# Weight splits of the up products in product order, each behind an evacuation three products back

## The chip, the cores and the metric

The kernel runs on one core of a Trainium2 chip. The metric is the device time of one execution in microseconds (us). The engines are TensorE (PE in the profile), VectorE (DVE), ScalarE (ACT), GpSimd (POOL) and SyncE (SP), each with its own in-order instruction stream; SP and GpSimd also issue the DMAs.

## The reference

One sequence of 512 rows and width 1024 goes through four layers, all in float32. The first two add a mixer (forgetting attention, then a gated recurrence) and a SwiGLU; the last two another pair of mixers and a convolutional FFN. Each FFN begins with an "up" GEMM from 1024 to 2 x 2816 columns; the change touches these four.

```
def swiglu_ffn(h, w_in, w_out):
    gate, up = jnp.split(jnp.einsum('bsd,df->bsf', h, w_in), 2, axis=-1)
    return jnp.einsum('bsf,fd->bsd', jax.nn.silu(gate) * up, w_out)

def conv_ffn(h, w_up, conv_w, conv_b, w_down):
    u = h @ w_up
    up = jnp.pad(u, ((0, 0), (CONV_WIDTH - 1, 0), (0, 0)))
    conv = conv_b
    for j in range(CONV_WIDTH):
        conv = conv + conv_w[j] * up[:, j:j + s]
    a, g = jnp.split(conv, 2, axis=-1)
    return (jax.nn.silu(a) * g) @ w_down
```

Before each FFN stands an RMS norm: the rows are divided by the root of the mean of their squares over the 1024 columns.

## The kernel before

Every float32 GEMM is done as three passes over split operands: a high part (a cast to the matmul's own type, `hi`) and a low part (`lo = raw - hi`). For weights, `pump` emits the splits in the order of a list of `Spec`s: a CAST on ScalarE (L237), a subtraction on VectorE (L238), and for some an adding DMA on GpSimd (L240), which adds another block of the weight from DRAM into the same raw tile, so that the next split of that tile is that of a sum. `pump` goes on as long as a slot (W0 to W2, and W3 during the up GEMMs) and the raw tiles are there.

The four up GEMMs (up0 and up1 for SwiGLU, up2 and up3 for the convolution; at about 300 to 540, 1020 to 1260, 1600 to 1845 and 2200 to 2445 us) are done for each pair of column tiles j (11 of them) by a scheme that needs seven products instead of eight. Products p1 and p2 use plain weight blocks, p5, p6, p3, p7, p4 blocks that are sums built up by the adding DMAs: p6 is cast from the raw tile of p5 after one such DMA, and so on. A product is 24 matmuls. `up_first` does p1 and p2 of j = 0 to 3 while the last norm still runs; `up` then does pairs (0,1) and (2,3), and from j = 4 a loop: p5(j), p1(j+1), p3(j), p6(j), p2(j+1), p7(j), p4(j). p3 accumulates on the PSUM bank of p5, and p7 on that of p6; so p3 waits until ScalarE has copied p5's result out (L904 in SwiGLU, L947 in conv), and p7 until it has copied p6's (L906, L949).

The evacuations (`swiglu_evac`, `conv_evac`) are the copies and adds that assemble the outputs: copies on ScalarE, adds on VectorE (L908, L951, L957) and GpSimd (L915, L954); in conv then the convolution (ScalarE `u` and `s`, L931, VectorE L932 and L933), a silu (L962) and a product on GpSimd (L965). Names in the trace: `W` is a split slot, `raw` a raw tile, `hid` the outputs, `a`, `s`, `g`, `m` the activations' splits and PSUM banks.

The order of PE's instructions is written by hand. On the other engines a scheduler lists the instructions by readiness and priority when the kernel is built; `high_priority` raises some of them.

`norm_chain` makes the norm in front of each FFN in two halves of 256 rows: VectorE updates `h` in four pieces of two column blocks, ScalarE squares each (L435), VectorE adds up the first three (L437), and `rstd` multiplies what is left as four operands (two halves of `sums`, two of the last square) with a vector of 1/1024 on PE (L399). `combine` then makes, for the second half, the sums of the activations (s1 to s4, a22) and their splits, in a fixed sequence on VectorE.

Of the kernel before, what the change touches and what calls it, by code (L numbers as in the profile page):

```python
# [8 lines left out]
F32 = mybir.dt.float32  # L9
# [49 lines left out]
class Spec:  # L59
# [1 line left out]

    def __init__(self, tag, nk, nc, slots, early, raw, loads=(), prep=None, add=None, ends=()):
        self.tag, self.nk, self.nc, self.slots, self.early = tag, nk, nc, slots, early
        self.raw, self.loads, self.prep, self.add, self.ends = raw, loads, prep, add, ends


class Net:
    def __init__(self, ctx, tc, t):  # L70
        self.ctx, self.tc, self.nc, self.t = ctx, tc, tc.nc, t
        nc = tc.nc
        e = ctx.enter_context
        self.base = e(tc.tile_pool(name="base", bufs=1))
        self.wp = e(tc.tile_pool(name="wp", bufs=1))
        self.nrm = e(tc.tile_pool(name="nrm", bufs=2))
        self.sm = e(tc.tile_pool(name="sm", bufs=4))
        self.psg = e(tc.tile_pool(name="psg", bufs=4, space=PSUM))
        self.psa = e(tc.tile_pool(name="psa", bufs=2, space=PSUM))
        self.psm = e(tc.tile_pool(name="psm", bufs=2, space=PSUM))  # L80
        self.drp = e(tc.tile_pool(name="drp", bufs=2, space=bass.MemoryType.DRAM))

        b = self.base
        self.h = b.tile([P, NC, S], F32, tag="h", name="h")
        self.ident = b.tile([P, P], F32, tag="ident", name="ident")
        make_identity(nc, self.ident)
        self.invn = b.tile([P, 1], F32, tag="invn", name="invn")
        nc.vector.memset(self.invn, 1.0 / D)
        self.mhalf = b.tile([P, 32], F32, tag="mhalf", name="mhalf")
        nc.vector.memset(self.mhalf, -0.5)  # L90
        self.slot_at = {f"W{i}": self.wp.tile([P, 2048], F32R, tag=f"W{i}", name=f"W{i}") for i in range(3)}
        self.free = {"W0", "W1", "W2"}
        self.raw_at = {f"raw{i}": self.wp.tile([P, 1024], F32, tag=f"raw{i}", name=f"raw{i}") for i in range(3)}
        self.raw_free = list(self.raw_at)
        self.raws = {}
        self.specs, self.loads = [], []
        self.adds, self.hold = [], False
        self.n_dma = self.n_split = self.n_got = self.n_raw = 0
        self.pe_time, self.later, self.events = 0.0, [], set()
        self.loaded = {}  # L100
# [116 lines left out]
    def pump(self, most=99):  # L217
        nc = self.nc
        for _ in range(most):
            if self.n_split == len(self.specs):  # L220
                break
            self.load_more()
            s = self.specs[self.n_split]
            slot = next((x for x in s.slots if x in self.free), None)
            if slot is None or any(k not in self.raws for k in s.loads):
                return
            if any(key in s.loads for key, *_ in self.adds):
                self.flush(self.last_pow)
            self.free.discard(slot)
            if s.prep:  # L230
                out, x, y, eng = s.prep
                getattr(nc, eng).tensor_add(self.raws[out][1], self.raws[x][1], self.raws[y][1])
            n = s.nk * s.nc
            reg = self.slot_at[slot]
            hi, lo = reg[:, :n], reg[:, 1024 : 1024 + n]
            raw = self.raws[s.raw][1][:, :n]
            nc.scalar.copy(hi, raw)  # L237
            (nc.gpsimd if s.early else nc.vector).tensor_sub(lo, raw, hi.bitcast(F32))  # L238
            if s.add is not None:
                nc.gpsimd.dma_start(raw.rearrange("p (k c) -> p k c", k=s.nk), s.add, accum_op=ALU.add)  # L240
            for k in s.ends:
                self.raw_free.append(self.raws.pop(k)[0])
            r = dict(k=s.nk)
            self.loaded[self.n_split] = Chunk(
                slot, hi.rearrange("p (k c) -> p k c", **r), lo.rearrange("p (k c) -> p k c", **r), s.nk)
            self.n_split += 1
        self.load_more()
# [142 lines left out]
            nc.scalar.activation(sq[:, :n], src, AF.Square)  # L390
            eng.tensor_add(acc[:, cols], acc[:, cols], sq[:, :n])  # L391

    def rstd(self, parts):

        nc = self.nc
        st = self.mbank()
        for j in range(2):
            for i, a in enumerate(parts):
                nc.tensor.matmul(st[:, j : j + 1], a[:, j * P : (j + 1) * P], self.invn, start=i == 0,  # L399
                                 stop=i == len(parts) - 1)  # L400
        with self.tc.high_priority(400):
            v = self.sm.tile([P, 2], F32, tag="v", name="v")
            nc.vector.tensor_scalar_add(v, st[:, 0:2], EPS)
            r = self.sm.tile([P, 2], F32, tag="r", name="r")
            self.last_pow = nc.gpsimd.tensor_tensor(r, v, self.mhalf[:, 0:2], ALU.pow)
        return r
# [9 lines left out]
    def norm_chain(self, acc, half, gain, pool=None, y=None, acc_y=None, work=None):  # L416


        nc = self.nc
        cols = slice(half * HS, (half + 1) * HS)  # L420
        if y is not None:
            yield 2.6
            r = self.rstd([acc_y[:, cols]])
            if half and work is not None:
                self.flush(self.last_pow)
            yield 2.0
            R = self.spread(r)[:, :HS].unsqueeze(1).to_broadcast([P, 2, HS])
            with self.tc.high_priority(400):
                sums = pool.tile([P, 2, HS], F32, tag="sums", name="sums", bufs=2)
                for c in range(0, NC, 2):  # L430
                    tmp = y[:, c : c + 2, cols]
                    hv = self.h[:, c : c + 2, cols]
                    nc.vector.tensor_mul(tmp, tmp, R)
                    (nc.vector.tensor_sub if work is None else nc.vector.tensor_add)(hv, hv, tmp)
                    nc.scalar.activation(tmp if c else sums, hv, AF.Square)  # L435
                    if c in (2, 4):
                        nc.vector.tensor_add(sums, sums, tmp)  # L437
            parts = [a[:, i] for a in (sums, tmp) for i in range(2)]
            yield 7.0
        else:  # L440
            yield 5.4 if half and work is not None else 2.6
            parts = [acc[:, cols]]
        r = self.rstd(parts)
        if half and work is not None:
            self.flush(self.last_pow)
        yield 1.4 if y is not None else 2.8 if half and work is not None else 2.0
        R = self.spread(r)
        with self.tc.high_priority(400):
            if work is not None:
                with self.tc.manual_schedule(engines={mybir.EngineType.DVE}):  # L450
                    self.combine(pool, work, half, gain, R)
                return
            for c in range(NC):
                tmp = self.nrm.tile([P, HS], F32, tag="tmp", name="tmp", bufs=3)
                nc.vector.scalar_tensor_tensor(tmp, self.h[:, c, cols], gain[:, c : c + 1], R[:, :HS], ALU.mult,
                                               ALU.mult)
                self.split(tmp, self.res(c, 0, half), self.res(c, 1, half))

    def combine(self, pool, work, half, gain, R):
# [19 lines left out]
        if not half:  # L479
            rest = []  # L480
            for c in range(NC):
                norm(c)
                rest.append(high("a12" if c >= 4 else "a11", c % 4, work[:, c, cols], 1))
                if c > 1:
                    rest.pop(0)()
            for low in rest:
                low()
            return
        g = (0, 2)
        a11, a12 = [work[:, k : k + 2, lo] for k in g], [work[:, 4 + k : 6 + k, lo] for k in g]  # L490
        a21, a22 = [work[:, k : k + 2, hi] for k in g], [work[:, 4 + k : 6 + k, hi] for k in g]
# [19 lines left out]
        s2[1]()  # L511
        s3 = [high("s3", g[i], a21[i]) for i in range(2)]
        last = [high("a22", g[i], a22[i]) for i in range(2)]
        for low in s3 + last:
            low()


    def columns(self, pool):
# [232 lines left out]
    def plan_up(self, tag, w, engines=None):  # L751
# [11 lines left out]

        def spec(j, p, raw, **kw):
            slots = early[j > 0] if (j, p) in first else W[:3] if (j, p) in rest[-3:] else W
            self.specs.append(Spec(tag, 4, 256, slots, False, raw, **kw))

        for j, p in first + rest:
            e = j < self.EARLY
# [55 lines left out]
    def up_first(self, tag, st):  # L825

        st["x"], st["y"], st["c11"] = {}, {}, {}
        for j, p in self.up_order()[0]:
# [3 lines left out]
            else:  # L832
                st["y"][j] = self.abank()
                self.product(tag, p, st["y"][j])
                if j < 2:
                    c = st["c11"][j] = self.nrm.tile([P, S], F32, tag="sq", name="c11")
                    self.c11(st["x"][j], st["y"].pop(j), c)

    def c11(self, x, y, out):
        self.nc.scalar.copy(out, x)  # L840
# [2 lines left out]
    def up(self, tag, st, evac):  # L843
# [9 lines left out]
        for j, p in rest:  # L853
# [25 lines left out]
            done.add((j, p))  # L879
            if p in (3, 6) and {(j, 3), (j, 6)} <= done:  # L880
                first(j, 3, z.pop(j))

    @staticmethod
    def halves(a):
# [1260 lines left out]
```

## Time and profile before

| | us |
|---|---|
| median of 3 runs | 2580.16 |
| lowest, highest | 2576.74, 2585.74 |
| profiled execution | 2584.16 |
| its span | 2582.3 |

In the span PE is busy 96%, the weight loads (PEld, beside it) 85%, VectorE 59%, ScalarE 45%, GpSimd 21%. Of the chain that ended last 43% lies on PE, 6% on VectorE, 3% on DMA and 2% on ScalarE. The rows further down are from the timelines, where a row is start, duration, engine, line, operation, output<-inputs, shapes, count, and in brackets the idle time of the engine before it and what ended that; and from a table of stretches.

### The profile page before, as it was taken

To read this page: it belongs to the slowest core of one execution; us is meant where nothing else is said; L and a number is where in the kernel's file an instruction comes from. 1 tells how busy PE (TensorE), PEld (TensorE's weight loads), DVE (VectorE), ACT (ScalarE), POOL (GpSimd) and SP (SyncE) were. 2 spreads that over 40 slices of the span, in tenths; PEclk is the share of its full clock that TensorE was granted. 3 is DMA by queue.
4 is the path that set the end of the run, shared out by engine and by line. 5 is a ranking of instruction groups with operands and counts; after the bars stand their busy time and mean duration, and the time that the engine had idled before them with its cause. 6 is when DMAs were issued, how large, how long until landed. Compare 5 with 4: busy or idle time off the path is not lost.

```text
span 2582.3 us, 40752 instructions
## 1 busy us (share of the span) xinstructions
PE 2467.4 (96%) x16477; PEld 2205.8 (85%) x16477; DVE 1527.4 (59%) x2400; ACT 1168.2 (45%) x1920; POOL 550.1 (21%) x500
## 2 busy tenths in 40 slices
PE   8999889999999998799999989899999999999999
PEld 6778889998898988799988759899888768989978
DVE  5766565563555555655625675787834445697841
ACT  4545445553232324455533553566622433466731
POOL 0000133310011111233101221455300000264400
PEclk9999989999999999899999999999999999999999
DMA  4223379944112123799531213989541223889741
GB/s 136 83 74 99 105 136 191 184 108 127 50 58 74 58 90 94 142 191 186 111 127 62 65 58 106 160 172 175 119 129 57 65 58 106 181 167 177 146 142 29
DMA packets 304886, 297.00 MB, mean 115 GB/s; under 512 B 11645, under 2 KB 294875, under 8 KB 304699
## 3 DMA queue, kind: packets, MB, share of 16 engines
q1 hardware_dynamic: 210235, 197.57, 25.0%
q0 software_dynamic: 94384, 96.81, 24.1%
q8 instruction: 129, 2.11, 0.3%
q14 instruction: 58, 0.48, 0.1%
q10 hardware_dynamic: 80, 0.03, 0.0%
HBM read 292.24 MB, written 2.13 MB: 114 GB/s over the span
## 4 chain that ended last, share of the span: by engine, by line
PE 43%; DVE 6%; DMA 3%; issue 3%; ACT 2%; POOL 1%; ACTq 0%; DVEq 0%; POOLq 0%
PE g L334 34%; PE a L334 4%; DMA raw<-in_ffn_w_up_dram 3%; DVE W L238 2%; ACT W L237 1%; PE m L334 1%; PE m L1900 1%; DVE u L932 1%; DVE s L932 1%; DVE s L933 0%; ACT s L931 0%; PE a L1883 0%; PE a L1209 0%; DVE R L173 0%; DVE u L933 0%
## 5 line engine op out<-in xcount | busy, mean ns | idle before, releaser
L238 DVE TENSOR_TENSOR W<-raw,W 128x1024 fp32r<-128x1024 f32 x455 | 573.2, 1263 | 458.9 <-ACT W L237 456.1
L237 ACT CAST W<-raw 128x1024 fp32r<-128x1024 f32 x455 | 472.4, 1040 | 603.6 <-PE g L334 272.7
L334 PE MATMUL g<-R,W 128*128 128x512 f32 (+2 forms) x3048 | 685.0, 375 | 7.8 <-DVE W L238 4.8
L334 PEld LDWEIGHTS g<-R,W 128*128 128x128 f32 (+1 forms) x3048 | 511.4, 190 | 105.1 <-issue 6.1
L334 PE MATMUL g<-s,W 128*128 128x256 f32 x3840 | 479.2, 284 | 27.6 <-ACT hid L947 13.6
L334 PEld LDWEIGHTS g<-s,W 128*128 128x128 f32 x3840 | 467.9, 191 | 32.5 <-ACT hid L947 16.5
L334 PE MATMUL g<-W,R 128*128 128x256 f32 (+1 forms) x1224 | 233.9, 337 | 0.0
L334 PEld LDWEIGHTS g<-W,R 128*128 128x128 f32 x1224 | 181.8, 191 | 25.3 <-issue 6.7
L334 PE MATMUL a<-a,W 128*128 128x256 f32 x1536 | 196.1, 283 | 3.5 <-DVE c L841 2.2
L334 PEld LDWEIGHTS a<-a,W 128*128 128x128 f32 x1536 | 188.8, 190 | 4.3 <-DVE c L841 2.4
L240 POOL DMA_DIRECT2D raw<-in_ffn_w_in_dram x78 | 100.4, 1289 | 228.5 <-DVE W L238 212.4
L240 POOL DMA_DIRECT2D raw<-in_ffn_w_up_dram x78 | 103.5, 1368 | 121.5 <-DVE W L238 114.5
L334 PE MATMUL g<-a,W 128*128 128x256 f32 x864 | 109.6, 282 | 0.3
L965 POOL TENSOR_TENSOR hid<-u,s 128x512 f32<-128x512 f32 x44 | 82.6, 1887 | 118.4 <-ACT s L962 111.8
L334 PE MATMUL g<-R,R 128*128 128x256 f32 (+1 forms) x792 | 107.0, 291 | 0.7 <-ACT ya L657 0.7
L334 PEld LDWEIGHTS g<-a,W 128*128 128x128 f32 x864 | 105.6, 189 | 1.1 <-DVE a L475 0.9
L238 DVE TENSOR_TENSOR X<-raw,X 128x1024 fp32r<-128x1024 f32 (+1 forms) x46 | 49.6, 1085 | 95.6 <-ACT X L237 95.6
L391 POOL TENSOR_TENSOR acc<-acc,sq 128x512 f32<-128x512 f32 x19 | 30.0, 1581 | 355.1 <-ACT sq L390 355.0
L334 PEld LDWEIGHTS g<-R,R 128*128 128x128 f32 x792 | 101.2, 195 | 2.7 <-ACT ya L657 1.1
L334 PE MATMUL g<-R,X 128*128 128x256 f32 (+1 forms) x576 | 94.0, 320 | 0.0
L334 PEld LDWEIGHTS g<-R,X 128*128 128x128 f32 x576 | 83.1, 190 | 7.8
L237 ACT CAST X<-raw 128x1024 fp32r<-128x1024 f32 (+1 forms) x46 | 42.9, 937 | 98.6 <-PE g L334 72.3
(413 smaller groups left out, 3451.2 us busy)
## 6 DMA issues: line engine op xcount, KB each, us to landing
raw<-in_ffn_w_in_dram POOLq DMA_DIRECT2D x88, 512.0 KB, 6.3
raw<-in_ffn_w_up_dram POOLq DMA_DIRECT2D x88, 512.0 KB, 6.3
raw<-in_ffn_w_in_dram SPq DMA_DIRECT2D x76, 512.0 KB, 4.9
raw<-in_ffn_w_up_dram SPq DMA_DIRECT2D x76, 512.0 KB, 4.8
raw<-in_ffn_w_out_dram SPq DMA_DIRECT2D x40, 512.0 KB, 3.5
raw<-in_ffn_w_down_dram SPq DMA_DIRECT2D x40, 512.0 KB, 4.0
raw<-in_hgrn_w_in_dram SPq DMA_DIRECT2D x32, 512.0 KB, 4.1
raw<-in_fox_w_in_dram SPq DMA_DIRECT2D x24, 512.0 KB, 3.8
```

Of the source, the lines that this page charges most:

```text
L237: nc.scalar.copy(hi, raw)
L238: (nc.gpsimd if s.early else nc.vector).tensor_sub(lo, raw, hi.bitcast(F32))
L240: nc.gpsimd.dma_start(raw.rearrange("p (k c) -> p k c", k=s.nk), s.add, accum_op=ALU.add)
L334: self.nc.tensor.matmul(*args, **kw, **(dict(skip_group_check=True) if skip else {}))
L391: eng.tensor_add(acc[:, cols], acc[:, cols], sq[:, :n])
L932: nc.vector.scalar_tensor_tensor(u[:, 1:], src[:, : S - 1], w(1), u[:, 1:], ALU.mult, ALU.add)
L965: nc.gpsimd.tensor_mul(hid[:, t], u, s)
L1900: mm(po[i * 64 : i * 64 + 64, h * HS : (h + 1) * HS], q[:, 2 * b + h, ck * 64 : (ck + 1) * 64], state[h], start=True, stop=True)
```

## The change

A `Spec` of an up GEMM carries `up`, and for the products 4 to 7 `summed`. p3's block, a plain one, isn't counted as summed.

- `pump` stops at a summed split while `n_split > n_evac + 3`. `n_evac` is set to `n_got - 1` in the new `evacuated()`, which is called behind each product's evacuation and pumps again.
- The CASTs of the up splits are chained in product order on ScalarE (`issue_after`), and the subtractions get the priority 200.
- In `norm_chain` VectorE adds all three later squares and then the two halves of the sum into `acc`; `rstd` takes this one operand.
- `combine` hands the low parts of s3 and a22 back to be issued behind it, outside its priority and its fixed sequence.

```
@@ pump
             if slot is None or any(k not in self.raws for k in s.loads):
                 return
+            if s.summed and self.n_split > self.n_evac + 3:
+                return
@@
-            nc.scalar.copy(hi, raw)
-            (nc.gpsimd if s.early else nc.vector).tensor_sub(lo, raw, hi.bitcast(F32))
+            with self.tc.issue_after(self.last_hi.ins) if s.up and self.last_hi else ExitStack():
+                self.last_hi = nc.scalar.copy(hi, raw)
+            with self.tc.high_priority(self.FIRST) if s.up else ExitStack():
+                (nc.gpsimd if s.early else nc.vector).tensor_sub(lo, raw, hi.bitcast(F32))
@@ rstd
-            for i, a in enumerate(parts):
-                nc.tensor.matmul(st[:, j : j + 1], a[:, j * P : (j + 1) * P], self.invn, start=i == 0,
-                                 stop=i == len(parts) - 1)
+            nc.tensor.matmul(st[:, j : j + 1], acc[:, j * P : (j + 1) * P], self.invn, start=True, stop=True)
@@ norm_chain
-                    if c in (2, 4):
+                    if c:
                         nc.vector.tensor_add(sums, sums, tmp)
-            parts = [a[:, i] for a in (sums, tmp) for i in range(2)]
+                nc.vector.tensor_add(acc[:, cols], sums[:, 0], sums[:, 1])
@@ combine
-        for low in s3 + last:
-            low()
+        return s3 + last
@@ plan_up
-            self.specs.append(Spec(tag, 4, 256, slots, False, raw, **kw))
+            self.specs.append(Spec(tag, 4, 256, slots, False, raw, up=True, summed=p > 3, **kw))
@@ up_first, up: behind each product's evacuation
+            self.evacuated()
+    def evacuated(self):
+        self.n_evac = self.n_got - 1
+        self.pump()
```

In the loop of up2, ScalarE's rows of one group before, from the cast of p5 to the copy that p3 waits for. In order the casts are those of p5, p1, p3, p6 and p2.

```order
L237 CAST W3_14896<-raw3_14904 128x1024
L949 COPY hid_14900<-g_15890 128x2x256
L237 CAST W2_90<-raw5_14906 128x1024
L237 CAST W0_88<-raw2_93 128x1024
L953 COPY g_16002<-g_15890 128x2x256
L237 CAST W1_89<-raw3_14904 128x1024
L931 ACTIVATE u_16290<-hid_14900,ccol_409 128x512
L931 ACTIVATE u_16300<-hid_14900,ccol_409 128x512
L931 ACTIVATE s_16285<-g_16002,ccol_409 128x512
L931 ACTIVATE s_16295<-g_16002,ccol_409 128x512
L237 CAST W3_14896<-raw4_14905 128x1024
L947 COPY hid_14900<-g_16305 128x2x256
```

The same place in the changed kernel (L243 is the CAST, L962 the copy of p6, L966 of p7, L960 of p5):

```order
L962 COPY hid_14868<-g_15858 128x2x256
L243 CAST W1_89<-raw3_14872 128x1024
L243 CAST W3_14864<-raw5_14874 128x1024
L243 CAST W2_90<-raw2_93 128x1024
L966 COPY g_15964<-g_15858 128x2x256
L243 CAST W0_88<-raw3_14872 128x1024
L944 ACTIVATE u_16255<-hid_14868,ccol_409 128x512
L944 ACTIVATE u_16265<-hid_14868,ccol_409 128x512
L944 ACTIVATE s_16250<-g_15964,ccol_409 128x512
L944 ACTIVATE s_16260<-g_15964,ccol_409 128x512
L243 CAST W1_89<-raw4_14873 128x1024
L960 COPY hid_14868<-g_16270 128x2x256
```

The copy of p6 now stands ahead of p5's CAST, and that CAST goes to W1 (the slot that p2 reads) instead of W3 (that of p6); W3 now takes p1. The rest keeps its order.

In the beginning of up2, ScalarE's rows around the two c11 copies before:

```order
L237 CAST W0_88<-raw1_92 128x1024
L390 ACTIVATE sq_14613<-h_78 128x256
L237 CAST W1_89<-raw2_93 128x1024
L390 ACTIVATE sq_14617<-h_78 128x256
L840 COPY c11_14678<-g_14620 128x512
L237 CAST W2_90<-raw0_91 128x1024
L840 COPY c11_14782<-g_14681 128x512
L474 CAST a22_14187<-yb_14195 128x2x256
```

The same place after:

```order
L243 CAST W0_88<-raw1_92 128x1024
L397 ACTIVATE sq_14581<-h_78 128x256
L243 CAST W1_89<-raw2_93 128x1024
L397 ACTIVATE sq_14585<-h_78 128x256
L852 COPY c11_14641<-g_14588 128x512
L852 COPY c11_14747<-g_14644 128x512
L243 CAST W2_90<-raw0_91 128x1024
L481 CAST a22_14155<-yb_14163 128x2x256
```

The CAST of the first summed split has moved behind the second c11 copy.

## Rows read from the trace of the kernel before

**Rows 1.** Stretches: start:end, us, busy PE PEld DVE ACT POOL, PEclk, DMA share, GB/s

```profile
280.00:380.00 100.00, 81.55 (x592) 80.21 (x591) 62.17 (x99) 44.76 (x72) 19.84 (x17) 0.86 0.63 138
...
1000.00:1100.00 100.00, 81.92 (x594) 79.68 (x593) 62.89 (x97) 45.16 (x72) 25.04 (x20) 0.88 0.70 147
1600.00:1720.00 120.00, 109.34 (x860) 107.11 (x859) 96.05 (x112) 66.09 (x90) 55.84 (x37) 0.96 0.87 174
1720.00:1840.00 120.00, 116.49 (x971) 115.46 (x970) 96.91 (x111) 79.89 (x109) 56.02 (x38) 1.00 0.86 163
2200.00:2320.00 120.00, 109.25 (x894) 106.80 (x893) 98.20 (x119) 67.84 (x93) 55.28 (x36) 1.00 0.88 177
2320.00:2440.00 120.00, 115.99 (x967) 114.97 (x965) 97.28 (x111) 79.05 (x107) 57.18 (x39) 1.00 0.88 166
```

**Rows 2.** Timeline of TensorE in the loop of up2, one group of products

```profile
1729.63 5.98 PE L334 MATMUL g<-s,W 128*128 128x256 f32 x48 [0.15 <-ACT hid L947]
1735.45 3.01 PE L334 MATMUL a<-a,W 128*128 128x256 f32 x24
1738.30 3.02 PE L334 MATMUL g<-s,W 128*128 128x256 f32 x24
...
1750.61 1.57 PE L334 MATMUL g<-s,W 128*128 128x256 f32 x11 [0.73 <-ACT hid L947]
```

**Rows 3.** Timeline of ScalarE in the same group

```profile
1735.53 1.05 ACT L237 CAST W<-raw 128x1024 fp32r<-128x1024 f32 x1 [0.51 <-PE g L334]
...
1745.25 1.05 ACT L237 CAST W<-raw 128x1024 fp32r<-128x1024 f32 x1 [2.44 <-DMA raw<-in_ffn_w_up_dram]
...
1749.98 0.57 ACT L947 COPY hid<-g 128x512 f32<-128x512 f32 x1
```

**Rows 4.** Timeline of VectorE in the same group

```profile
1736.62 2.15 DVE L238 TENSOR_TENSOR W<-raw,W 128x1024 fp32r<-128x1024 f32 x1 [1.34 <-ACT W L237]
...
1739.88 1.21 DVE L238 TENSOR_TENSOR W<-raw,W 128x1024 fp32r<-128x1024 f32 x1
```

**Rows 5.** Timeline of GpSimd in the same group

```profile
1734.65 3.03 POOL L965 TENSOR_TENSOR hid<-u,s 128x512 f32<-128x512 f32 x2 [6.48 <-ACT s L962]
1739.06 1.30 POOL L240 DMA_DIRECT2D raw<-in_ffn_w_up_dram  x1 [1.39 <-DVE W L238]
```

**Rows 6.** Timeline of TensorE behind idle stretches of up0, up1 and up2

```profile
370.02 7.50 PE L334 MATMUL g<-s,W 128*128 128x256 f32 x48 [2.90 <-ACT hid L906]
...
1082.77 5.99 PE L334 MATMUL g<-s,W 128*128 128x256 f32 x48 [2.73 <-ACT hid L906]
...
1716.20 4.63 PE L334 MATMUL g<-s,W 128*128 128x256 f32 x24 [2.30 <-ACT hid L949]
```

**Rows 7.** Timelines of TensorE, GpSimd and ScalarE in the loop of up0

```profile
451.53 3.02 PE L334 MATMUL g<-s,W 128*128 128x256 f32 x24
...
462.94 1.23 PE L334 MATMUL g<-s,W 128*128 128x256 f32 x9
...
451.36 1.28 POOL L240 DMA_DIRECT2D raw<-in_ffn_w_in_dram  x1 [9.40 <-DVE W L238]
...
457.64 1.05 ACT L237 CAST W<-raw 128x1024 fp32r<-128x1024 f32 x1 [1.60 <-DMA raw<-in_ffn_w_in_dram]
...
460.22 1.05 ACT L237 CAST W<-raw 128x1024 fp32r<-128x1024 f32 x1 [0.87 <-PE g L334]
461.17 0.58 ACT L904 COPY hid<-g 128x512 f32<-128x512 f32 x1
```

**Rows 8.** Timelines of TensorE and VectorE at the second rstd of up0

```profile
328.66 0.98 PE L399 MATMUL m<-invn,sums 128*128 128x1 f32 x4 [8.25 <-DVE sums L437]
...
332.07 2.48 PE L334 MATMUL g<-a,R 128*128 128x256 f32 x10
...
327.83 0.68 DVE L437 TENSOR_TENSOR sums<-sums,yb 128x512 f32<-128x512 f32 x1
```

**Rows 9.** Timeline of ScalarE in the beginning of up2

```profile
1616.13 1.05 ACT L237 CAST W<-raw 128x1024 fp32r<-128x1024 f32 x1 [10.92 <-DMA raw<-in_ffn_w_up_dram]
```

More of the change, by code (lines that the diff above doesn't have):

```diff
@@ L59, with __init__ @@
 class Spec:
-    def __init__(self, tag, nk, nc, slots, early, raw, loads=(), prep=None, add=None, ends=()):
+    def __init__(self, tag, nk, nc, slots, early, raw, loads=(), prep=None, add=None, ends=(), up=False,
+                 summed=False):
         self.tag, self.nk, self.nc, self.slots, self.early = tag, nk, nc, slots, early
         self.raw, self.loads, self.prep, self.add, self.ends = raw, loads, prep, add, ends
+        self.up, self.summed = up, summed
 class Net:
@@ L97, in __init__ @@
         self.adds, self.hold = [], False
+        self.last_hi, self.n_evac = None, 0
         self.n_dma = self.n_split = self.n_got = self.n_raw = 0
@@ L391, in add_square, with rstd @@
             eng.tensor_add(acc[:, cols], acc[:, cols], sq[:, :n])
-    def rstd(self, parts):
+    def rstd(self, acc):
         nc = self.nc
@@ L422, in norm_chain @@
             yield 2.6
-            r = self.rstd([acc_y[:, cols]])
+            r = self.rstd(acc_y[:, cols])
             if half and work is not None:
@@ L441, in norm_chain @@
             yield 5.4 if half and work is not None else 2.6
-            parts = [acc[:, cols]]
-        r = self.rstd(parts)
+        r = self.rstd(acc[:, cols])
         if half and work is not None:
@@ L447, in norm_chain @@
         R = self.spread(r)
+        if work is not None:
+            with self.tc.high_priority(400):
+                with self.tc.manual_schedule(engines={mybir.EngineType.DVE}):
+                    rest = self.combine(pool, work, half, gain, R)
+            for low in rest:
+                low()
+            return
         with self.tc.high_priority(400):
[L449 to L452, printed above, removed]
             for c in range(NC):
@@ L487, in combine @@
                 low()
-            return
+            return []
         g = (0, 2)
@@ L881, in up @@
                 first(j, 3, z.pop(j))
+            self.evacuated()
     @staticmethod
```

## The prediction

> **What bounds the kernel now.** I read the page's busy shares first, then a table of busy time by stretch, then the timelines of the engines at the places where TensorE (PE) waits. The four up GEMMs are where the diff acts. [rows 1] cuts each into a beginning and a steady end: in its 100 or 120 us beginning PE is idle 100 − 81.55 = 18.5 us (up0), 18.1 (up1), 10.7 (up2) and 10.8 (up3); in the steady ends of up2 and up3 it is idle for 3.5 and 4.0 us, and in up0's a p3 follows without idle time [rows 7]. So PE sets the end nearly everywhere. A new wait of PE costs its full length, and there is more to win in the beginnings than in the loops. Two things must therefore be weighed: what the gate does to a loop that hardly waits now, and what the new orders give back in the beginnings.
>
> **The gate in the loop of up2 and up3.** One group of seven products is p3, p6, p2, p7, p4, p5, p1. In [rows 2] p3 and p6 of one group start at 1729.63, p2 at 1735.45, p7 at 1738.30, and p3 of the next group at 1750.61: a period of 20.98 us. One product is 1738.30 − 1735.45 = 2.85 us, seven are 19.97, so the group loses 1.0 us, 0.73 of it as idle before p3, which waits for ScalarE's copy of p5 (L947). That copy stands at the end of a chain that begins with p5's split: ScalarE casts p5 at 1735.53 [rows 3], VectorE starts the low part at 1736.62 and takes 2.15 us [rows 4], GpSimd issues the adding DMA at 1739.06 [rows 5], and ScalarE can cast p6 out of the same raw tile at 1745.25, 6.19 us after the issue [rows 3]. Behind that CAST in ScalarE's order stand two u, two s, the CAST of p2 and L947, which is done in time for PE at 1750.61: 5.36 us. This chain already sets p3's start. Its head, the cast of p5, follows the end of p6 (p2 starts at 1735.45) by 0.08 us.
>
> After the change the same chain stands in the same order, but its head is later. The order of the changed kernel puts that CAST into W1, which p2 has to leave first, and W3 goes to the next p1. p2 ends where p7 starts, 8.67 us after p3; p6 ended 5.82 us after p3. The head moves by one product, 2.85 us. From p3's start T: CAST at T + 8.75, its low part 1.09 later at the earliest, the adding DMA 0.29 behind the low part's end, 6.19 to the CAST of p6, 5.36 to p3. What is not known is VectorE's share. Lower end: VectorE free and 1.21 us, as in the undisturbed row [rows 4]: T + 8.75 + 1.09 + 1.21 + 0.29 + 6.19 + 5.36 = T + 22.9. Upper end: an add of the evacuations ahead of it (0.68, the length of an add in [rows 8]) and 2.15 as beside GpSimd's L965 (1734.65 to 1737.68, [rows 5]): T + 24.5. I take one add ahead and 1.21, T + 23.6, since L965's pair comes ahead of the split in the new order. Against 20.98 that is 2.6 us a group (1.9 to 3.5). There are four such groups in a layer (j = 5 to 8) and two layers: **+21 us** (15 to 28).
>
> Nothing else that the gate delays costs here: p5 itself runs two products after p2, and its CAST and low part need about 3 us of 5.7. The other SP loads start later by as much, under cover of the same products.
>
> PE's clock. [rows 6] show the idle stretches of the beginnings with what came after. After 2.30 us idle at 1716.20 a product took 4.63 us where it takes 3.02 [rows 2]: 1.6 us at the lower of the clock's two levels. After 2.90 us idle at 370.02, 48 matmuls took 7.50 us, after 2.73 idle at 1082.77 only 5.99. So a new idle of this size can cost 1.6 us more, or nothing. I charge 3 of the 8: **+5** (0 to 13).
>
> By the Trainium skill, "DMA: Bandwidth & Descriptors", section "Anatomy of one DMA — SWDGE (gpsimd) path", a DMA that GpSimd issues takes about 2.0 us and the bytes at 436 GB/s; by that figure 512 KB would be an estimate of 3.2 us. The row says 6.19, in a stretch in which the 16 DMA engines are 86% busy [rows 1], so the row decides. By the page's figure the chain would end at T + 20.5, nearly covered.
>
> **The gate in the loop of up0 and up1.** The same group, with fewer steps behind the CAST of p6. In [rows 7] the DMA is issued at 451.36, the CAST of p6 starts at 457.64 (6.28 later), a silu follows, ScalarE then idles 0.87 us until p5 has left the slot of p2's CAST (460.22), copies p5 (L904) until 461.75, and p3 starts at 462.94 with no idle of PE. The cover is 0.87 + 1.19 = 2.1 us. After the change the CAST of p5 follows the end of p2 (p7 starts at 451.53) instead of p6. At that moment VectorE has the two or three adds of this point ahead of the low part, which in the new order stand first: CAST at 451.6, low part from 452.7 to 454.2, issue at 454.45, 3.1 us later than now. 3.1 − 2.1 = 1.0 us a group. With VectorE free it would be 0.8, with three more adds in the way about 2.6. Some 11 groups of both layers: **+11 us** (4 to 20). These idles are too short to be charged with a slow clock.
>
> **VectorE sums the squares.** rstd has one operand instead of four. In [rows 8] PE waits 8.25 us for the last sum, and the matmuls of rstd then take from 328.66 to 332.07, 3.41 us. A quarter of them is left, 0.85 us. Against that VectorE must add the last square (0.68) and then the two halves (256 wide; at most the same): about 1.1 us later. 3.41 − 0.85 − 1.1 = 1.5 us. The 8.25 us themselves stay: the same CASTs stand ahead of the squares on ScalarE. There are eight such places; three are like this one and the others, whose matmuls run at full clock or hide beside other work, give 0 to 1: **−6 us** (−3 to −7).
>
> **The beginnings.** In up0 and up1 the p7 of the first pair waits 2.90 and 2.73 us for L906 [rows 6], since ScalarE stands at a CAST whose adding DMA went out late, behind another tile's. With the splits in product order that DMA goes first and L906 is reached in time; with the slow clock behind the first, 2.90 + 1.5 + 2.73 = 7.1, and some 3 us of shorter waits for W3 before it: **−10 us** (−4 to −13). In up2, ScalarE stands 10.92 us at a CAST whose data is not there [rows 9], with the second c11 copy and the normalised activations behind it. In the new order the c11 copy comes ahead of that CAST, and the low parts of s3 and a22 no longer stand in VectorE's fixed sequence; of PE's 10.7 us idle here with its slow products I expect 8 back (3 to 12), of up3's 10.8 only 4 (0 to 8), since its waits are for L947 and L949 as in the loop: **−12 us** (−3 to −20).
>
> **The sum.** 21 + 5 + 11 − 6 − 10 − 12 = +9 us. The profiled execution took 2584.16 us, 4.0 above the median of the runs shown (2580.16); both get the same sum, so 2593 for one like it, and 2589 for the median. All losses at their upper and all gains at their lower end would be 61 − 10 = +51, the reverse 19 − 40 = −21.
>
> **The rivals.**
> 1. **The beginnings win.** PE is idle 58 us in the four beginnings [rows 1], of which about 16 are the two waits for the sums. If the product order takes away half of the other 42 (21), some 5 of its slow clock, and 6 come from the rstd matmuls, 32 in all, against a loop at its lower ends (15 + 4), the time is about 2567. For it: every one of these waits is for something that stands behind a CAST that was issued too early, as in [rows 9], and that is what the gate forbids. Against it: the adding DMA keeps its 6 us, and with only three products of lead it starts later in the beginnings too. It decides from the point where the beginnings give back more than 37 us with the sums.
> 2. **The two halves cancel.** The loop's losses at 30, the gains at 28: 2582, no difference. For it: all terms are of one size.
> 3. **Every new idle costs clock too.** If all 8 idles of up2 and up3 are followed by a slow product (13 us) and VectorE is occupied when p5's low part is due (28 and 18): 59 − 25 = +34 gives 2614. For it: in up2's beginning the idle at 1716.20 was followed by one. Against: the row at 1082.77.
> 4. **The DMA lands sooner.** A loop that waits moves less per us, and the 6.19 and 6.28 us shrink. Were they 3 us shorter, both loops would lose nothing and 28 us of gains would stay: 2553. The page named above would have it so; every landing in these rows speaks against it.
>
> **How the numbers follow.** My forecast (its own range 2582 to 2601) has a chance of 0.40, rival 3 0.18, rival 2 0.13, rival 1 0.25, rival 4 0.04. About 0.3%, 7.7 us, is what a measurement of this kernel can tell from no change, so slower begins at 2587.9 and faster ends at 2572.4. Of the forecast's 0.40 I put 0.28 above 2587.9. Slower is then 0.28 + 0.18 = 0.46, within 0.12 + 0.13 = 0.25, faster 0.25 + 0.04 = 0.29. The range for 8 in 10 reaches into rivals 1 and 3, 2564 to 2616, and leaves out rival 4 and the outer parts of these two.
>
> **What would show it.** In the profile after, the steady windows of up2 and up3 should show periods of p3 of 23 to 24 us instead of 20.98, with PE idle 2 to 4 us before p3 for the copy of p5; the CAST of p5 just behind the end of p2; the steady end of up0 no longer free of idle time but with about 1 us before p3. rstd should take under 1 us of PE after the long wait, which stays near 8. p7's wait at up0's first pair should be gone. I am wrong if p3's period stays at 21 (then p5's split isn't held back by p2, or the DMA lands sooner), or if the beginnings of up0 and up1 together lose less than 25 us instead of the 36.5 they lose now.

## The result, and the profile after

The changed kernel takes 2624.99 us (median of 4 runs, 2623.85 to 2626.0) against 2578.45 us of the kernel before beside it: a ratio of 1.0174 with a 95% interval of 1.0154 to 1.0194. It is 46.5 us slower. The prediction was 2589 with a range of 2564 to 2616: the sign is right, the time lies outside.

The profiled execution of the changed kernel has a span of 2621.7 us, 39.4 more than before, with PE's busy time hardly changed (2470.4 us, before 2467.4). So 36 us of the difference are PE standing idle. The busy time is a balance: the matmuls of rstd take 14.5 us instead of 30.0, and products at a lower clock, which come up below, add to it. The table of PE's waits shows for what (engine, tile and line waited for: us in total, times, longest):

```profile
PE g L341 <- ACT hid L960: 39.0, 15, 4.1
PE m L405 <- DVE acc L443: 36.9, 7, 9.1
PE g L341 <- ACT hid L917: 12.6, 13, 2.8
...
PE g L341 <- ACT hid L962: 2.1, 3, 1.4
...
PE g L341 <- ACT hid L919: 0.9, 2, 0.7
```

The same view of the kernel before, where L947, L904, L949 and L906 are the copies that are now L960, L917, L962 and L919, and the sums are L437 instead of L443:

```profile
PE m L399 <- DVE sums L437: 24.8, 6, 8.3
PE g L334 <- ACT hid L947: 13.6, 14, 1.9
PE g L334 <- ACT hid L949: 8.2, 5, 2.4
PE g L334 <- ACT hid L906: 5.6, 2, 2.9
...
PE m L334 <- ACT hid L947: 2.4, 4, 1.0
```

The copies of p6 (L962, L919) are hardly waited for any more, 3.0 us instead of 13.8. The copies of p5 are: 39.0 us in up2 and up3 instead of 16.0, and 12.6 us in up0 and up1, where PE did not wait for them at all.

For an account by stages I took the first and the last copy of p6 in each up GEMM, as one view lists them (line, engine, operation, count: shortest, median and longest in ns, first and last start). Here up2 before and after:

```profile
L949 ACT COPY hid<-g x11: 573/577/581, 1647.4 to 1835.8; 128x512 f32<-128x512 f32 x11
```

```profile
L962 ACT COPY hid<-g x11: 561/578/582, 1643.1 to 1852.0; 128x512 f32<-128x512 f32 x11
```

From the first to the last of them, which is the pairs and the loop, up2 takes 208.9 us instead of 188.4. All four:

| first to last copy of p6, us | up0 | up1 | up2 | up3 |
|---|---|---|---|---|
| before | 174.5 | 173.1 | 188.4 | 187.5 |
| after | 182.7 | 183.0 | 208.9 | 209.2 |
| difference | +8.2 | +9.9 | +20.5 | +21.7 |

That is 60.3 us. Up to the first copy in each stage (from the last copy of the stage before) the changed kernel gains 8.7, 11.4 and 2.3 us in up0, up1 and up2 and loses 0.8 in up3: 21.6 gained. Behind the last copy 0.7 is lost. 60.3 − 21.6 + 0.7 = 39.4, the difference of the spans.

TensorE in the loop of up2 after, which answers to [rows 2] (start, duration, engine, line, operation, count, idle time before and what ended it):

```profile
1727.29 7.48 PE L341 MATMUL g<-s,W 128*128 128x256 f32 x48 [4.10 <-ACT hid L960]
...
1751.67 7.47 PE L341 MATMUL g<-s,W 128*128 128x256 f32 x48 [2.63 <-ACT hid L960]
...
1775.93 7.52 PE L341 MATMUL g<-s,W 128*128 128x256 f32 x48 [2.52 <-ACT hid L960]
...
1786.16 3.04 PE L341 MATMUL g<-s,W 128*128 128x256 f32 x24
...
1800.98 8.56 PE L341 MATMUL g<-s,W 128*128 128x256 f32 x48 [3.15 <-ACT hid L960]
...
1827.60 7.37 PE L341 MATMUL g<-s,W 128*128 128x256 f32 x48 [3.79 <-ACT hid L960]
```

Two things are to be seen. The idle time before p3 is 2.5 to 4.1 us, as forecast. And behind every one of them the 48 matmuls of p3 and p6 take 7.4 to 8.6 us instead of 5.98 [rows 2], part of them at the lower of the clock's two levels. The table of stretches shows it for the group at 1775.93 (start:end, length, busy PE PEld DVE ACT POOL, granted clock, DMA share, GB/s): 0.55 of full speed in its first 2.5 us.

```profile
1775.90:1778.40 2.50, 2.47 (x12) 2.48 (x13) 2.50 (x4) 0.45 (x1) 0.00 (x0) 0.55 1.14 178
```

The periods are 24.38, 24.26, 25.05 and 26.62 us, on average 25.1; before, the same four were 21.1 on average. In up3 it is the same: idle times of 2.5 to 4.1 us, 7.3 to 8.0 us behind each, periods of 24.7 us on average (20.9 before).

ScalarE, VectorE and GpSimd in the group that begins at 1775.93, which answer to [rows 3], [rows 4] and [rows 5]:

```profile
1786.29 2.00 ACT L243 CAST W<-raw 128x1024 fp32r<-128x1024 f32 x2 [1.39 <-issue]
...
1795.63 1.05 ACT L243 CAST W<-raw 128x1024 fp32r<-128x1024 f32 x1 [4.98 <-DMA raw<-in_ffn_w_up_dram]
...
1800.36 0.57 ACT L960 COPY hid<-g 128x512 f32<-128x512 f32 x1
```

```profile
1786.26 0.68 DVE L964 TENSOR_TENSOR hid<-g,hid 128x512 f32<-128x512 f32 x1
1786.86 0.68 DVE L956 TENSOR_TENSOR g<-a,g 128x512 f32<-128x512 f32 x1
1787.45 2.35 DVE L245 TENSOR_TENSOR W<-raw,W 128x1024 fp32r<-128x1024 f32 x2
```

```profile
1789.30 2.61 POOL L247 DMA_DIRECT2D raw<-in_ffn_w_up_dram  x2 [4.04 <-DVE W L245]
```

p5's CAST starts at 1786.29, just behind the end of p2 (p7 starts at 1786.16) and 10.36 us after p3. From the CAST to the next p3 (1800.98) the chain takes 14.7 us; the prediction had 8.75 for the one and 14.8 for the other. So the chain behind the CAST was put right. Its head is 1.6 us later than forecast, since p3 and p6 ran at the slow clock in between.

### The profile page after: what moved, and what is told of

Same layout as the page of the kernel before. It is cut to its first block, busy times and chain, and to the rows that moved or that the text cites. A ratio compares the mean times of both kernels' runs of the same rounds, so it can differ in the third digit from the quotient of the medians.

```text
span 2621.7 us, 40536 instructions
## 1 busy us (share of the span) xinstructions
PE 2470.4 (94%) x16381; PEld 2207.5 (84%) x16381; DVE 1521.1 (58%) x2416; ACT 1164.4 (44%) x1920; POOL 531.8 (20%) x500
## 3 DMA queue, kind: packets, MB, share of 16 engines
q0 software_dynamic: 94384, 96.81, 23.6%
## 4 chain that ended last, share of the span: by engine, by line
PE 63%; issue 13%; DMA 10%; DVE 7%; ACT 5%; POOL 2%; ACTq 0%; POOLq 0%; SPq 0%; DVEq 0%
PE g L341 50%; DMA raw<-in_ffn_w_in_dram 6%; DMA raw<-in_ffn_w_up_dram 4%; PE a L341 3%; DVE W L245 2%; ACT W L243 2%; PE m L341 1%; PE a L1222 1%; POOL hid L978 1%; PE a L1467 1%; PE m L1467 1%; PE a L1509 1%; POOL raw L247 1%; PE m L1913 1%; ACT u L944 0%
## 5 line engine op out<-in xcount | busy, mean ns | idle before, releaser
L245 DVE TENSOR_TENSOR W<-raw,W 128x1024 fp32r<-128x1024 f32 x455 | 566.1, 1255 | 473.1 <-ACT W L243 466.4
L243 ACT CAST W<-raw 128x1024 fp32r<-128x1024 f32 x455 | 468.3, 1040 | 628.0 <-PE g L341 321.3
L341 PE MATMUL g<-s,W 128*128 128x256 f32 x3840 | 495.9, 290 | 55.8 <-ACT hid L960 39.0
L341 PEld LDWEIGHTS g<-s,W 128*128 128x128 f32 x3840 | 482.5, 196 | 63.8 <-ACT hid L960 42.0
L341 PEld LDWEIGHTS g<-W,R 128*128 128x128 f32 x1224 | 181.6, 191 | 25.9 <-issue 7.4
L247 POOL DMA_DIRECT2D raw<-in_ffn_w_in_dram x78 | 107.3, 1420 | 256.6 <-DVE W L245 232.5
L243 ACT CAST X<-raw 128x1024 fp32r<-128x1024 f32 (+1 forms) x46 | 42.8, 937 | 100.7 <-PE g L341 72.5
```

What stands on the lines that cost most here:

```text
L243: self.last_hi = nc.scalar.copy(hi, raw)
L341: self.nc.tensor.matmul(*args, **kw, **(dict(skip_group_check=True) if skip else {}))
```

## The experiments

Theory A: the gate moves p5's CAST in the loops by one product, which makes PE idle before p3, and the slow clock behind that idle time makes it worse; the product order of the casts and the rest of the change gain. Theory B: the casts' order or the priority does the harm. All ratios are against the kernel before on the same chip, with 95% intervals.

**Lead of four.**

```
-            if s.summed and self.n_split > self.n_evac + 3:
+            if s.summed and self.n_split > self.n_evac + 4:
```

> The changed kernel with one number of the gate changed: a summed split may run four products ahead of the last evacuation instead of three. Theory A (the gate makes p5's cast one product late, and the slow clock behind the new waits adds to it): the cast follows the end of p6 again, the period of p3 in the loop of up2 falls from 24.3 to 26.6 us back to about 21, the loops of up0 and up1 lose their 18 us, and what the beginnings gave stays: about 2555 to 2570 us. Theory B (the losses come from the casts' fixed order or the priority of the low parts): both are still there, the period stays at 24 or more, 2615 to 2630 us.

2568.44 us, 0.9953 (0.9938 to 0.9968). TensorE at p3 in the loop of up2:

```profile
1756.83 5.97 PE L341 MATMUL g<-s,W 128*128 128x256 f32 x48 [0.53 <-ACT hid L960]
...
1777.61 5.97 PE L341 MATMUL g<-s,W 128*128 128x256 f32 x48 [0.52 <-ACT hid L960]
```

The period is 20.78 us, a little under that of before. One more product of lead is worth 57 us. Theory B falls: order and priority are both in this kernel, and by themselves they do no harm.

**The slot given back first.**

```
             slot = next((x for x in s.slots if x in self.free), None)
+            if s.up and slot is not None:
+                slot = min((x for x in s.slots if x in self.free), key=lambda x: self.freed.get(x, -1))
...
         self.free.add(chunk.slot)
+        self.freed[chunk.slot] = self.n_got
```

> The changed kernel with its lead of three, but a split of the up products takes the free slot that was given back first, not the first one in the list. So p5's cast goes into the slot that p6 left, while the gate still holds it back in the program until p2's evacuation. If it is the reuse of p2's slot that makes the cast late, the period of p3 falls to about 21 us, as with a lead of four: 2555 to 2575 us. If it is the place that the gate gives the cast, the period stays at 24 or more and the time at 2615 to 2630.

2563.8 us, 0.9944 (0.9927 to 0.996), with the lead still at three. PE and ScalarE in the loop of up2:

```profile
1752.91 5.97 PE L345 MATMUL g<-s,W 128*128 128x256 f32 x48 [0.48 <-ACT hid L964]
1758.72 3.03 PE L345 MATMUL a<-a,W 128*128 128x256 f32 x24
...
1773.74 5.96 PE L345 MATMUL g<-s,W 128*128 128x256 f32 x48 [0.58 <-ACT hid L964]
```

```profile
1758.80 1.05 ACT L246 CAST W<-raw 128x1024 fp32r<-128x1024 f32 x1
```

The CAST stands behind the end of p6 again (p2 starts at 1758.72), as before the change. So what makes it late is not that the gate lets it into the program later, but what it then finds. In the changed kernel two slots are free at that moment: W1, which p2 has just left in the program, and W3, which p1 left before p3 (the order shown with the change has p1 in W3 and p6 in W0). The list of slots names W1 first, and in W1 the CAST must wait on the chip for p2's last matmul. With the slot given back first the one that it gets is p6's, and the gate costs the loop nothing: the four periods of up2 take 83.3 us, before 84.3.

**The gate in the beginnings only.**

```
-            ..., up=True, summed=p > 3, **kw))
+            ..., up=True, summed=p > 3 and j < self.EARLY, **kw))
```

> The changed kernel with the gate only for the splits of j = 0 to 3, the beginnings. Theory A: the loops are back at about 21 us a period and the beginnings as after the change, 2555 to 2570 us. If the gate is also what gave the beginnings their gain, this is faster than a kernel with a lead of four by up to 10 us; if the casts' order gave it, both are the same.

2558.67 us, 0.9913 (0.9897 to 0.993). Its loops have idle times of 0.5 to 0.8 us before p3 in up2, and from the first to the last copies of p6 it loses 10.3 us instead of 60.3. Up to the first copies it gains 7.8, 10.1, 8.5 and 9.5 us: in up2 and up3 18 us, where the changed kernel has 1.5.

**Filling the idle time.** 20 matmuls whose result nobody reads, ahead of p3 in eight groups:

```
             elif p == 3:
+                if self.EARLY < j < 9 and tag in ("up2", "up3"):
+                    self.fill(20)
                 self.product(tag, p, z[j], False)
...
+    def fill(self, n):
+        t = self.mbank()
+        for i in range(n):
+            self.nc.tensor.matmul(t[:, :HS], self.xop("a11", 0, 0)[:, :P], self.xop("a11", 0, 1), start=i == 0,
+                                  stop=i == n - 1)
```

> The changed kernel with 20 matmuls without use (2.4 us at full clock) set ahead of p3 in the eight loop groups of up2 and up3, where TensorE is idle for 2.5 to 4.1 us. If the slow clock behind these waits follows from TensorE's idling, the 48 matmuls behind it take 5.9 us instead of 7.4 to 8.6, p2 ends that much earlier, and with it all that follows: 12 to 30 us less than the changed kernel, 2595 to 2613 us. If the slow clock has another cause, nothing is gained: 2620 to 2630.

2615.02 us, 1.0132 (1.0112 to 1.0153), 10 us less than the changed kernel's median, a gain a little under what was expected. TensorE in the loop of up2:

```profile
1751.43 2.56 PE L850 MATMUL m<-a 128*128 128x256 f32 x20
1754.34 5.97 PE L341 MATMUL g<-s,W 128*128 128x256 f32 x48 [0.35 <-ACT hid L969]
...
1777.07 5.97 PE L341 MATMUL g<-s,W 128*128 128x256 f32 x48
...
1826.02 7.48 PE L341 MATMUL g<-s,W 128*128 128x256 f32 x48 [5.61 <-ACT hid L969]
```

With the idle time filled the 48 matmuls take 5.96 or 5.97 us in all eight filled groups, and the period is 22.97, 22.73 and 23.10 us (in up3 23.06, 22.91 and 22.75). The last row is the next group, which has no filler: 5.61 us idle, and 7.48 us again. The slow clock follows from the idle time: eight of eight groups have it without the filler, none with it. The two parts of the loop's loss come apart here. Over both stages the period is 21.0 us before, 24.9 in the changed kernel and 22.9 with the filler: 1.9 us a group stay with the clock kept up, 2.0 us are the clock's. The whole time gains less than 8 x 2.0 us, since the group behind the last filled one is later (5.61 us idle, where the changed kernel has 3.79).

**The gate alone**, added to the kernel before, with nothing else of the change.

```
+            if s.summed and self.n_split > self.n_evac + 3:
+                return
...
+            self.evacuated()
```

> The kernel before with nothing of the change but the gate with its lead of three. Theory A, as the runs so far leave it: the gate by itself makes p5's cast one product late, and the loops lose the 42 us of up2 and up3 and the 18 us of up0 and up1 that the changed kernel shows; the gain of the beginnings is absent or smaller. 2620 to 2645 us. If the gate needs the casts' fixed order to do harm, the time stays at 2575 to 2595.

2619.2 us, 1.0152 (1.0126 to 1.0177); a little below the expected range. From the first to the last copy of p6 its stages take 4.7, 12.7, 20.7 and 22.9 us more than before, 61 in all. That is the sum of the changed kernel, but not in the same places. The eight groups of up2 and up3 (j = 5 to 8) cost 9 us here and 31 there; 26 us lie ahead of them, in the pairs and j = 4, where in up2 PE waits once for the copy of p6:

```profile
1660.96 4.96 PE L338 MATMUL g<-s,W 128*128 128x256 f32 x24 [4.96 <-ACT hid L960]
...
1768.77 5.97 PE L338 MATMUL g<-s,W 128*128 128x256 f32 x48 [1.17 <-ACT hid L958]
...
1777.42 3.01 PE L338 MATMUL g<-s,W 128*128 128x256 f32 x24
...
1790.42 5.96 PE L338 MATMUL g<-s,W 128*128 128x256 f32 x48 [1.41 <-ACT hid L958]
```

```profile
1777.55 1.05 ACT L241 CAST W<-raw 128x1024 fp32r<-128x1024 f32 x1 [1.35 <-issue]
...
1783.83 1.52 ACT L942 ACTIVATE u<-hid,ccol 128x512 f32<-128x512 f32 x2 [1.95 <-POOL hid L965]
1786.48 1.05 ACT L241 CAST W<-raw 128x1024 fp32r<-128x1024 f32 x1 [1.13 <-DMA raw<-in_ffn_w_up_dram]
```

p5's CAST is behind the end of p2 in this kernel too (1777.55; p7 starts at 1777.42). But ScalarE does the two u ahead of the CAST of p6, so that from that CAST to p3 it is 3.9 us instead of 5.4. In up2's groups of j = 6 to 8 the idle time is then 1.2 to 1.4 us, and no slow product follows it. So the gate alone puts the CAST late; what that costs the loop depends on the rest of the change. Which part of the rest makes the difference wasn't tested. Up to the first copies the gate alone gains 25.9 us, 21.5 of them in up2 and up3. So the two kernels come out nearly level with different sums.

**VectorE's sums alone**, and the kernel with the early gate without them.

```
-                    if c in (2, 4):
+                    if c:
                         nc.vector.tensor_add(sums, sums, tmp)
-            parts = [a[:, i] for a in (sums, tmp) for i in range(2)]
+                nc.vector.tensor_add(acc[:, cols], sums[:, 0], sums[:, 1])
```

> The kernel before with nothing of the change but VectorE's sums of the squares. By the prediction's term: 6 us less than the kernel before, 2573 us. By the trace after the change, in which TensorE waits 36.9 us for the sums at seven places instead of 24.8 at six, with the matmuls of rstd a quarter: no difference within 4 us, 2575 to 2583.

> The kernel with the gate for the beginnings only, and the squares summed as before. If VectorE's sums give 6 us, this is 2564 us or so; if they give nothing, it is 2555 to 2561 like the one with them; if they cost, it is the fastest so far, 2550 to 2555.

The first takes 2582.38 us, 1.0011 (0.9995 to 1.0026), the second 2558.24 us, 0.9916 (0.9889 to 0.9942), beside 2558.67 with the sums. They give nothing that can be measured, not 6 us. The pair with the early gate shows where it goes. With the sums the matmuls of rstd take 14.4 us in all instead of 28.4, and PE waits 34.0 us for the sums instead of 21.9: 14.0 us are saved and 12.1 come back as waiting, 1.0 to 2.9 us at each of seven places. In the changed kernel, at the place of [rows 8]:

```profile
329.21 0.99 PE L405 MATMUL m<-invn,acc 128*128 128x1 f32 x4 [9.09 <-DVE acc L443]
330.06 2.27 PE L341 MATMUL g<-a,R 128*128 128x256 f32 x9
```

PE waits 9.09 us instead of 8.25 and is through with rstd 2.0 us earlier in the span, about as forecast. In the norm behind the down GEMM at 1380 us, before, after, and with the sums alone:

```profile
1382.30 1.83 PE L334 MATMUL g<-tail,W 128*128 128x256 f32 x14
1383.97 0.51 PE L399 MATMUL m<-invn,sums 128*128 128x1 f32 x4
...
1385.68 1.43 PE L334 MATMUL g<-tail,W 128*128 128x256 f32 x10
```

```profile
1379.83 1.83 PE L341 MATMUL g<-tail,W 128*128 128x256 f32 x14
1385.84 0.98 PE L405 MATMUL m<-invn,acc 128*128 128x1 f32 x4 [4.19 <-DVE acc L443]
1386.69 2.48 PE L341 MATMUL g<-tail,W 128*128 128x256 f32 x10
```

```profile
1370.48 1.83 PE L334 MATMUL g<-tail,W 128*128 128x256 f32 x14
1373.34 0.58 PE L398 MATMUL m<-invn,acc 128*128 128x1 f32 x4 [1.03 <-DVE acc L436]
1373.78 1.43 PE L334 MATMUL g<-tail,W 128*128 128x256 f32 x10
```

From the first row to the last it was 3.4 us; with the sums alone it is 3.3, though PE waits 1.03 us where the sums used to be ready. I had given such places 0 to 1 us of gain. In the changed kernel it is 6.9: PE waits 4.19 us and runs on at the slow clock. That loss isn't the sums' own; where it comes from stays open.

**What makes the beginnings faster.** Three parts taken away one by one from the kernel with the early gate, and the gate taken away from the changed kernel.

```
-            with self.tc.issue_after(self.last_hi.ins) if s.up and self.last_hi else ExitStack():
+            with ExitStack():
                 self.last_hi = nc.scalar.copy(hi, raw)
```

> The kernel with the gate for the beginnings only, without the fixed product order of the casts on ScalarE. If that order gives the gain of the beginnings (the p7 of the first pair, the copies ahead of the waiting casts), most of the 20 us against the kernel before goes: 2570 to 2582. If the gate and the priority of the low parts give it, the time stays at 2555 to 2563.

```
-            ..., up=True, summed=p > 3, **kw))
+            ..., up=True, **kw))
```

> The changed kernel without the gate anywhere; the casts' order, the priority and the rest stay. If the gate in the beginnings gives some of their gain, this is slower than the kernel with the gate there (2558.7): 2563 to 2575 us. If the casts' order alone gives it, the two are the same, 2555 to 2562.

```
-                    rest = self.combine(pool, work, half, gain, R)
-            for low in rest:
-                low()
+                    for low in self.combine(pool, work, half, gain, R):
+                        low()
```

> The kernel with the gate for the beginnings only, and the low parts of s3 and a22 in VectorE's fixed sequence as before. By the prediction the late low parts share in what the beginnings of up2 and up3 give; without them it would be 2561 to 2568 us. If the order of the casts gives all of it, 2555 to 2561.

```
-            with self.tc.high_priority(self.FIRST) if s.up else ExitStack():
+            with ExitStack():
                 (nc.gpsimd if s.early else nc.vector).tensor_sub(lo, raw, hi.bitcast(F32))
```

> The kernel with the gate for the beginnings only, without the priority of the weights' low parts on VectorE. If the adding DMAs gain from an earlier low part, this is slower than with it: 2563 to 2572 us. If not, 2555 to 2561.

| kernel | us | ratio, interval |
|---|---|---|
| early gate, all else as changed | 2558.67 | 0.9913 (0.9897 to 0.993) |
| without the casts' order | 2576.36 | 0.9983 (0.9967 to 0.9999) |
| without the gate | 2575.48 | 0.9985 (0.9973 to 0.9997) |
| low parts of s3 and a22 as before | 2556.23 | 0.9907 (0.9881 to 0.9933) |
| without the priority | 2552.78 | 0.9889 (0.9868 to 0.9909) |

Neither the casts' order alone nor the early gate alone gives more than 4 or 5 us; the two together give 20. I had expected one of them to carry it, and 2563 to 2575 us without the gate, which is just missed. The late low parts and the priority give nothing; without the priority the time is, if anything, lower, though the intervals overlap.

**The two parts that carry it**, alone on the kernel before.

```
+            if s.summed and self.n_split > self.n_evac + 3:
+                return
...
+            with self.tc.issue_after(self.last_hi.ins) if s.up and self.last_hi else ExitStack():
+                self.last_hi = nc.scalar.copy(hi, raw)
...
+            ..., up=True, summed=p > 3 and j < self.EARLY, **kw))
```

> The kernel before with two things of the change alone: the casts of the up splits in product order, and the gate for j = 0 to 3. If these two make the whole gain, as the runs without one of the other three parts say, the time is that of those runs, 2550 to 2560 us. If the three parts cover for each other, some of the gain goes, 2562 us or more.

2558.91 us, 0.9914 (0.99 to 0.9928): the whole gain, and 23 us faster than the kernel before that it was measured with.

## Why the prediction was wrong in size

**The gate in the loop of up2 and up3** was right as a mechanism, from the slot to the copy that PE waits for. With the idle time filled, the period is 22.9 us; the lower end of the prediction was T + 22.9, the value taken T + 23.6. So the term of 21 us is worth 15 by the runs. A lead of four and another slot both remove it.

**PE's clock** is the step that failed. I charged 3 of the 8 idle times with 1.6 us, since [rows 6] show one idle time of 2.73 us without a slow product behind it. All of them were followed by one, at 1.3 to 2.6 us each (7.28 to 8.56 against 5.98), and it comes back in full, since p2's end, on which the next CAST waits, moves with it. By the runs it is 2.0 us a group, 16 us for the 8 groups, where I had 5. This was rival 3, at 2614, to which I gave 0.18. Its condition on VectorE did not hold: the low part of p5 took about 1.2 us (two in 2.35) behind two short adds.

**The ends of these loops** are a second step that failed: I put them at nothing. From the first to the last copy of p6 up2 and up3 lose 42.2 us, the eight groups 31 of them. The other 11 lie in the pairs and j = 4 (5.5) and in the last groups (5.4), which I left out of the sum; the p3 of j = 9 too is a slow product (the row at 1827.60, whose idle time belongs to the fourth period). Behind the last copy, the last product of up2 and of up3 waits for its split, here in up2 after:

```profile
1859.23 5.06 PE L341 MATMUL a<-a,W 128*128 128x256 f32 x22 [2.60 <-DVE W L245]
```

In return a wait of 2.3 us for the next split at this place is gone. Neither the gate alone nor the early gate shows the new wait.

**The gate in the loop of up0 and up1.** 1.0 us a group was right: the idle times before p3 are 0.2 to 2.8 us, 12.6 us in all, against a term of 11, and none is followed by a slow product:

```profile
500.48 5.96 PE L341 MATMUL g<-s,W 128*128 128x256 f32 x48 [1.52 <-ACT hid L917]
...
1231.79 5.96 PE L341 MATMUL g<-s,W 128*128 128x256 f32 x48 [2.81 <-ACT hid L917]
```

The two stages lose 18.1 us from the first to the last copy, 11.8 in the groups of j = 5 to 8 and 5.7 ahead of them, in the pairs and j = 4.

**VectorE's sums** were put at −6 us and give nothing. The later sum was charged with 1.1 us at three places; it costs 1.0 to 2.9 us of waiting at seven.

**The beginnings.** In up0 and up1 the wait of p7 is gone or short (0.74 us instead of 2.90), and up to the first copy of p6 20.1 us are gained, where I had 10 and a part of the 6. In up2 and up3 I expected 12, and 1.5 came: the c11 copy did move ahead of the waiting CAST, but the products behind the norm now wait for splits instead (0.7 to 0.9 us three times in up2, one of them with a slow product behind it), and what lies between the stages eats a part (the last product of the stage before, the norm at 1380 us). With the gate in the beginnings only, the same stretches gain 18 us. That the casts' order gains only together with the gate was not in the prediction at all; why it needs the gate is not shown. Neither sign that I named for being wrong came: p3's period did not stay at 21 us, and PE's idle time in the windows of up0's and up1's beginnings is 33.0 us (36.5 before).

**The page's figure for the DMA.** By the Trainium skill, "DMA: Bandwidth & Descriptors", section "Anatomy of one DMA — SWDGE (gpsimd) path", the DMA would land in about 3.2 us, an estimate. After the change the adding DMA is issued at 1789.30 and the CAST of p6 starts 6.3 us later, in a loop that waits more. The trace doesn't agree with the figure, and the row of before was the right one to take; rival 4 falls with it.

Against the sum, between the two profiled executions: the loops were put at 21 + 5 + 11 = 37 us and cost 60; the gains were put at 28 and are 21. That is a miss of 30 us, 16 of them in up2 and up3 (the clock 11 more, the ends 11 more, the gate 6 less), 7 in up0 and up1, and 7 in the gains. By the medians the miss is 36 us; the profiled execution before was itself 6 us above its median.

## What to carry to other kernels

A wait that comes back every period is worth its length and what the clock takes behind it, and where the next period hangs on the product that was slowed, it is worth both in full; if the trace shows the slow clock behind only some idle times of that size, the bound to plan with is all of them. The places that a sum leaves out, here the groups on either side of the loop, need a bound too. When a kernel is made to emit work later, look at which buffer the later work then gets: with the first free one in a fixed list it can be the one given back last, which is the only one still to be waited for. A limit on the look-ahead that helps where a stage begins, with its queues full of things not yet ready, should be tried there alone before it is put into the steady loop.

## What the runs showed of the hardware

Behind idle times of 2.5 to 4.1 us in a loop where PE is otherwise busy, the granted clock fell in every group of up2 and up3, and it did so too behind 1.82 us. At the same place of the kernel with the filler, where no filler stands, it did not fall behind 1.89 us (changed kernel, then the filler's):

```profile
1700.77 7.52 PE L341 MATMUL g<-s,W 128*128 128x256 f32 x48 [1.82 <-ACT hid L960]
```

```profile
1704.87 5.97 PE L341 MATMUL g<-s,W 128*128 128x256 f32 x48 [1.89 <-ACT hid L969]
```

Nor did it behind 2.81 us in up1 (the row at 1231.79 above). Length alone doesn't tell the two apart; what does, these runs leave open. 20 matmuls that fill the gap, their result unused, kept the clock up in every filled group of up2 and up3, once (2348.79 in up3) although 2.22 us of idle time were left behind them.
